# Fetching a block's V rows in turn with the next block's U rows

## The chip, the cores and the metric

The kernel runs on one core of a Trainium2 chip. Times are device microseconds (us) of one execution. The engines are PE (TensorE, matrix products; PEld is its weight load), DVE (VectorE), ACT (ScalarE), POOL (GpSimd) and SP (SyncE). SP issues the plain loads from HBM, POOL the indirect ones, which gather rows by an index; 16 DMA engines move both. Each engine runs its own instructions in the order in which they were placed, and waits for the others by semaphores.

## The reference

The reference is two model blocks, one after the other, over 256 tokens of width 1024. What matters here is the product-key retrieval that closes each layer of the first block. Every token picks 128 experts (8 heads of 16) out of 16384; its hidden vector is multiplied with the 128 rows `u_tab[e]`, and the results weigh the 128 rows `v_tab[e]`:

```python
def block(hb):                       # 128 tokens
    ...
    e = i1 * N_KEYS + i2             # n, 8 heads, 16 experts
    g = jax.nn.softmax(sc.astype(jnp.float32), axis=-1).astype(hb.dtype)
    a = jax.nn.gelu(jnp.einsum('nhkd,nd->nhk', u_tab[e], hb)) * g
    return jnp.einsum('nhk,nhkd->nd', a, v_tab[e])
```

In layer 0 it is done for the 256 latent tokens x and for the 256 context tokens xc; in layer 1 for x alone.

## The kernel before, in words

The kernel is unrolled. A scheduler orders each engine's instructions from the order of the program, so that code that is written in turn comes out roughly in turn. Layer 0's retrieval is `peer0`. It treats the two sets of tokens in two ways at once.

The latent tokens go densely. A main loop has 128 steps, called chunks here. Chunk c takes one tile of 512 KB of V (128 experts): ACT rounds it to `whi` (L349), DVE takes the rest `wlo` (L352), and PE adds 12 products into `ps_acc`. Until chunk 76 it takes one tile of U as well, 52 chunks ahead (`ps_U`, 8 products, then ACT's Gelu into `A`, L1377). The weights that pick the experts, `ps_G`, are made beside it on DVE and PE, in four bursts. A third strand, `ps_ada`, makes layer 1's modulations from loads `raw<-in_wada`. SP loads all these through four buffers `raw`.

The context tokens go by gathering, in the generator `gathered`, two blocks of 128 tokens. First come the dots: for each of 128 experts of a token, POOL gathers the row of U for the 128 tokens of the block into a buffer (L1289), and DVE multiplies it with the tokens' hidden vectors `ht` and sums (L1303). Then a Gelu, a product and a transpose give the weights `aT`. Last come the sums: for each token POOL gathers its 128 rows of V (512 KB as well), and PE multiplies them with a column of `aT` that DVE has put into `Z`, 4 products into `ps_gv`. After 32 tokens ACT copies `ps_gv` into `yg` (L1329), PE transposes it (`ps_gT`) and DVE adds it to the context.

The gathered rows go into a ring of buffers, `st["buf"]`: four `gb` to begin with, and the two tiles `ht` when the dots that read them are done. Gather number n takes buffer n modulo the length of the ring, and waits until that buffer's last reader is through. `peer0` calls the generator 2.1 times beside every chunk's U part and 2.1 times beside its V part (`UNITS`), so 4.2 steps a chunk until chunk 76 and 2.1 after it. There are 512 steps: 256 dots and 256 sums. Layer 1's `peer1` uses the same generator with one block.

Of the kernel before, what the change touches and what calls it, by code (L numbers as in the profile page):

```python
# [7 lines left out]
FT = mybir.dt.float32  # L8
# [3 lines left out]
OP = mybir.AluOpType  # L12
# [5 lines left out]
P = 128  # L18
# [278 lines left out]
class Kern:  # L297
# [995 lines left out]
    def gathered(self, st, l, s, nb):  # L1293


        nc, pe = self.nc, self.pe
        U, V = self.A[f"Ur{l}"], self.A[f"V{l}"].rearrange("a b d -> (a b) d")
        x = self.X if s else self.XC
        aT = []
        for b in range(nb):  # L1300
            for j in range(P):
                t = self.rows_of(st, U, st["e"][:, b, j:j + 1])
                nc.vector.scalar_tensor_tensor(t, t, 1.0, st["ht"][:, b], op0=OP.mult, op1=OP.mult,  # L1303
                                               accum_out=st["d"][:, b, j:j + 1])
                yield
            d = st["d"][:, b]
            nc.scalar.activation(d, d, AF.Gelu_apprx_tanh)
            nc.vector.tensor_mul(d, d, st["g"][:, b])
            ps = self.psb("ps_aT")
            self.tr(ps[:, 0:P], d)  # L1310
            a = pe.tile([P, P], FT, tag="aT", bufs=2, name="aT")
            nc.scalar.copy(a, ps[:, 0:P])
            aT.append(a)
        st["buf"] += [st["ht"][:, b] for b in range(nb)]
        for g in range(nb * P // 32):
            po = self.psb("ps_gv")[:, :256]
            for k in range(32):
                t = 32 * g + k
                if t % self.NZ == 0:
                    z = st["Z"][t // self.NZ % 2]  # L1320
                    nc.vector.tensor_copy(z[:, :, 32:33], aT[t // P][:, t % P:t % P + self.NZ].unsqueeze(2))
                v = self.rows_of(st, V, st["eT"][:, t // P, t % P:t % P + 1])
                for q in range(4):
                    self.mm(po[32 * q:32 * q + 32], z[:, t % self.NZ, 32 - k:64 - k], v[:, q * 256:(q + 1) * 256],
                            k == 0, k == 31)
                yield

            y = pe.tile([P, 256], FT, tag="yg", bufs=1, name="yg")
            nc.scalar.copy(y, po)  # L1329
            pt = self.psb("ps_gT")  # L1330
            for c in range(2):
                self.tr(pt[:, c * P:(c + 1) * P], y[:, c * P:(c + 1) * P])
            for c in range(2):
                m = self.mods[l][:, 40 + c:48:2, s:s + 1].broadcast_to([P, 4, 32])
                xv = x[:, c::2, 32 * g:32 * g + 32]
                r = pe.tile([P, 4, 32], FT, tag="rg", bufs=2, name="rg")
                nc.vector.tensor_tensor(r, pt[:, c * P:(c + 1) * P].rearrange("p (q t) -> p q t", q=4), m, op=OP.mult)
                nc.vector.tensor_tensor(xv, xv, r, op=OP.add)
        self.gathered_all = True
        yield  # L1340

# [987 lines left out]
```

## Time and profile before

| | us |
|---|---|
| median of three runs | 3970.74 |
| lowest and highest | 3969.45, 3972.92 |
| profiled execution, its own time | 3959.87 |
| span of its trace | 3958.1 |
| PE busy | 3552.3 (90%) |
| DVE busy | 2345.2 (59%) |
| POOL busy | 1253.4 (32%) |

The span is read in 40 slices of 99 us. `peer0`'s main loop lies between 975 and 1940 us, in slices 10 to 19 (counted from 0), and is followed by a short rest of gathers until about 1980 us. In that stretch the DMA engines are busy most of the time, and DVE is busy first and idle later. A granted clock below 1.00 means that PE ran a part of that stretch at the lower of its two levels.

### The profile page before, as it was taken

The numbers are of one execution on the slowest core, as the hardware profiler recorded it, in microseconds if no ns is written. First come the engines' busy times: TensorE is split into PE (matmuls) and PEld (weight loads), VectorE is DVE, ScalarE is ACT, GpSimd is POOL, SyncE is SP. The second block draws the span as 40 slices with busy tenths as digits, with TensorE's granted clock in tenths as the row PEclk, the third lists the DMA queues.
The fourth block names the chain that finished last, engine by engine and source line by source line (L and its number), as shares of the span: only waits on it lengthen the run. The fifth ranks groups of instructions, "written<-read, shape, count | busy, mean of one in ns | idle before, by whom it ended". The sixth has DMA issues, their size and how long they took to land. (4 is left out here: it accounts for less than half of the span.)

```text
span 3958.1 us, 63943 instructions
## 1 busy us (share of the span) xinstructions
PE 3552.3 (90%) x24642; PEld 2838.3 (72%) x24642; DVE 2345.2 (59%) x5406; ACT 1201.6 (30%) x2156; POOL 1253.4 (32%) x1037
## 2 busy tenths in 40 slices
PE   8999996967898799899889996777999999999999
PEld 6777875755676566566489995673334899999899
DVE  5843358789687643165377448854201656865785
ACT  5433321111111111123265411110001646554554
POOL 0012204532534534455513204534432132231122
PEclk9999998987898999999999998899999999999999
DMA  5244237974989989899924468999998404565354
GB/s 214 66 158 149 91 113 250 336 248 139 364 315 351 371 296 333 313 335 391 373 91 160 147 213 306 344 409 396 409 409 333 149 25 137 181 203 172 99 178 147
DMA packets 265793, 961.39 MB, mean 243 GB/s; under 512 B 29832, under 2 KB 31504, under 8 KB 265488
## 3 DMA queue, kind: packets, MB, share of 16 engines
q1 hardware_dynamic: 154752, 554.08, 40.1%
q0 software_dynamic: 110592, 402.70, 27.0%
q8 instruction: 194, 3.18, 0.3%
q14 instruction: 111, 0.91, 0.1%
q10 hardware_dynamic: 144, 0.52, 0.0%
HBM read 956.12 MB, written 1.06 MB: 242 GB/s over the span
## 5 line engine op out<-in xcount | busy, mean ns | idle before, releaser
L322 PE MATMUL ps_U<-h,raw 128*128 128x256 f32 (+1 forms) x4096 | 758.0, 342 | 63.8 <-DMA raw<-in_U 37.5
L322 PEld LDWEIGHTS ps_U<-h,raw 128*128 128x128 f32 x4096 | 657.7, 201 | 145.4 <-ACT A L1485 36.1
L352 DVE TENSOR_TENSOR wlo<-raw,whi 128x1024 fp32r<-128x1024 f32 (+1 forms) x409 | 503.4, 1232 | 420.1 <-ACT whi L349 418.6
L349 ACT CAST whi<-raw 128x1024 fp32r<-128x1024 f32 (+1 forms) x502 | 517.7, 1034 | 751.0 <-DMA raw<-in_V 340.4
L1289 POOL DMA_INDIRECT gb<-in_Ur,er x384 | 469.2, 1222 | 856.4 <-DVE gb L1303 441.0
L1303 DVE SCALAR_TENSOR_TENSOR gb<-gb,ht 128x1024 f32<-128x1024 f32 x384 | 466.3, 1226 | 223.3 <-DMA gb<-in_Ur,er 222.4
L352 POOL TENSOR_TENSOR wlo<-raw,whi 128x1024 fp32r<-128x1024 f32 (+1 forms) x93 | 222.0, 2387 | 929.0 <-ACT whi L349 733.0
L1289 POOL DMA_INDIRECT gb<-in_V,eT x280 | 291.9, 1042 | 329.9 <-PE ps_gv L322 286.3
L322 PE MATMUL ps_in<-hh_hi,whi 128*128 128x256 f32 (+1 forms) x776 | 267.2, 347 | 1.7 <-ACT hh_hi L567 1.7
L322 PE MATMUL ps_in<-hh_hi,wlo 128*128 128x256 f32 (+1 forms) x776 | 262.7, 339 | 1.1 <-POOL wlo L352 1.1
L322 PE MATMUL ps_in<-hh_lo,whi 128*128 128x256 f32 (+1 forms) x776 | 263.5, 340 | 0.1
L322 PE MATMUL ps_acc<-raw,A 128*128 128x512 f32 x512 | 256.1, 621 | 8.0 <-DMA raw<-in_V 7.8
L322 PE MATMUL ps_acc<-wlo,a_hi 128*128 128x512 f32 x512 | 216.7, 423 | 45.3 <-DVE wlo L352 45.1
L322 PE MATMUL ps_acc<-whi,a_hi 128*128 128x512 f32 x512 | 220.0, 437 | 12.4 <-ACT whi L349 12.4
L322 PE MATMUL ps_acc<-whi,a_lo 128*128 128x512 f32 x512 | 211.9, 414 | 0.0
L322 PE MATMUL ps_gv<-gb,Z 128*32 128x256 f32 x2240 | 172.5, 398 | 9.6 <-DMA gb<-in_V,eT 8.9
L322 PE MATMUL ps_q<-h,raw 128*128 128x256 f32 x768 | 176.3, 382 | 0.0
L322 PEld LDWEIGHTS ps_acc<-raw,A 128*128 128x128 f32 x512 | 86.5, 190 | 121.4 <-issue 78.8
L322 PEld LDWEIGHTS ps_in<-hh_hi,whi 128*128 128x128 f32 x776 | 147.7, 191 | 27.3 <-issue 8.4
L1289 POOL DMA_INDIRECT ht<-in_V,eT x104 | 111.8, 1075 | 163.3 <-PE ps_gv L322 143.1
L322 PEld LDWEIGHTS ps_in<-hh_hi,wlo 128*128 128x128 f32 x776 | 147.3, 190 | 19.4 <-POOL wlo L352 1.9
L322 PEld LDWEIGHTS ps_in<-hh_lo,whi 128*128 128x128 f32 x776 | 147.6, 190 | 15.8 <-DVE hh_lo L570 0.3
(627 smaller groups left out, 7335.5 us busy)
## 6 DMA issues: line engine op xcount, KB each, us to landing
raw<-in_U SPq DMA_DIRECT2D x256, 512.0 KB, 6.8
raw<-in_V SPq DMA_DIRECT2D x256, 512.0 KB, 7.5
raw<-in_win SPq DMA_DIRECT2D x96, 512.0 KB, 4.0
raw<-in_wup SPq DMA_DIRECT2D x88, 512.0 KB, 4.2
raw<-in_wada SPq DMA_DIRECT2D x80, 512.0 KB, 5.1
raw<-in_wq SPq DMA_DIRECT2D x48, 512.0 KB, 4.1
raw<-in_gwin SPq DMA_DIRECT2D x37, 512.0 KB, 3.5
raw<-in_wdn SPq DMA_DIRECT2D x32, 512.0 KB, 4.3
```

Of the source, the lines that this page charges most:

```text
L322: self.nc.tensor.matmul(o, l, r, start=start, stop=stop)
L349: nc.scalar.copy(hi[:, :f], raw[:, :f])
L352: eng.tensor_sub(lo[:, :f], raw[:, :f], hi[:, :f].bitcast(FT))
L1289: self.nc.gpsimd.indirect_dma_start(t, None, table, bass.IndirectOffsetOnAxis(ap=at, axis=0), bounds_check=P * P - 1, oob_is_err=False)
L1303: nc.vector.scalar_tensor_tensor(t, t, 1.0, st["ht"][:, b], op0=OP.mult, op1=OP.mult, accum_out=st["d"][:, b, j:j + 1])
```

## The change

`gathered` is cut into two inner generators, `dots(b)` and `sums(b)`. Block 0's dots run first, as before. Then one step of block 1's dots and one step of block 0's sums are taken in turn, 128 pairs. Then come block 1's sums. The numbers of gathers, of products and of steps stay what they were. `ht` of block 0 joins the ring after block 0's dots (five buffers), `ht` of block 1 after block 1's (six). With one block (`peer1`) nothing changes.

```diff
         aT = []
-        for b in range(nb):
+
+        def dots(b):
             for j in range(P):
                 t = self.rows_of(st, U, st["e"][:, b, j:j + 1])
...
             aT.append(a)
-        st["buf"] += [st["ht"][:, b] for b in range(nb)]
-        for g in range(nb * P // 32):
-            po = self.psb("ps_gv")[:, :256]
...
+            st["buf"].append(st["ht"][:, b])
+
+        def sums(b):
+            for g in range(4 * b, 4 * b + 4):
+                po = self.psb("ps_gv")[:, :256]
...
+        yield from dots(0)
+        last = sums(0)
+        for b in range(1, nb):
+            d = dots(b)
+            while True:
+                n = 0
+                for q in (d, last):
+                    if next(q, self) is not self:
+                        n += 1
+                        yield
+                if n == 0:
+                    break
+            last = sums(b)
+        yield from last
         self.gathered_all = True
```

What this does to the order on the engines is seen at three places. The first is POOL, where the gathers of the context stand one behind the other. `in_Ur` is the table of U's rows and `in_V` that of V's; `gb` and `ht` are the buffers. Before:

```order
L1289 DMA gb<-in_Ur,er 128x1024 x134
L1289 DMA ht<-in_V,eT 128x1024
L1289 DMA gb<-in_Ur,er 128x1024 x122
L1289 DMA gb<-in_V,eT 128x1024 x3
L1289 DMA ht<-in_V,eT 128x1024
```

And now:

```order
L1289 DMA gb<-in_Ur,er 128x1024 x129
L1289 DMA gb<-in_V,eT 128x1024
L1289 DMA gb<-in_Ur,er 128x1024 x2
L1289 DMA ht<-in_V,eT 128x1024
L1289 DMA gb<-in_V,eT 128x1024 x3
L1289 DMA ht<-in_Ur,er 128x1024
L1289 DMA gb<-in_Ur,er 128x1024 x2
L1289 DMA ht<-in_V,eT 128x1024
```

From the 130th on gathers of V stand among those of U: of the eleven shown behind the 129, six are of V, and fill buffers that only PE empties.

The second place is DVE just after the dots of block 0, at chunk 6: `dots<-dots,gr` is the product after that block's Gelu, `wlo`, `a_lo` and `adar` belong to the dense work. Before:

```order
L1308 TENSOR_TENSOR dots<-dots,gr 128x128
L1303 SCALAR_TENSOR_TENSOR gb,dots<-gb,ht 128x1024
L352 TENSOR_TENSOR wlo<-raw,whi 128x1024
L363 TENSOR_TENSOR a_lo<-A,a_hi 128x256
L1303 SCALAR_TENSOR_TENSOR gb,dots<-gb,ht 128x1024 x4
L363 TENSOR_TENSOR a_lo<-A,a_hi 128x256
L352 TENSOR_TENSOR wlo<-raw,whi 128x1024
L1303 SCALAR_TENSOR_TENSOR gb,dots<-gb,ht 128x1024 x2
```

And now:

```order
L1309 TENSOR_TENSOR dots<-dots,gr 128x128
L352 TENSOR_TENSOR wlo<-raw,whi 128x1024
L363 TENSOR_TENSOR a_lo<-A,a_hi 128x256
L1304 SCALAR_TENSOR_TENSOR gb,dots<-gb,ht 128x1024 x2
L363 TENSOR_TENSOR a_lo<-A,a_hi 128x256
L352 TENSOR_TENSOR wlo<-raw,whi 128x1024
L441 TENSOR_TENSOR adar<-adar,ps_ada 128x256
L363 TENSOR_TENSOR a_lo<-A,a_hi 128x256
L352 TENSOR_TENSOR wlo<-raw,whi 128x1024
L441 TENSOR_TENSOR adar<-adar,ps_ada 128x256
```

The order goes on like this until chunk 16: at the 15th `wlo` 160 dots stand behind DVE before and 131 now; at the 25th it is 179 and 145, at the 45th 256 and 187. The first `ps_gv` stands on PE at chunk 47 before and at chunk 17 now, in both cases just behind the transpose `ps_aT`.

The third place is PE at chunk 70, with `ps_gv` as the sums, `ps_gT` as the transpose that follows 32 tokens, and between these rows the 12 products `ps_acc` of a chunk. Before:

```order
L322 MATMUL ps_gv<-gb,Z_3989 32x256 x8
L322 MATMUL ps_U<-h_3864,raw 128x256 x8
L327 MATMUL ps_gT<-cst,yg 128x128 x2
L322 MATMUL ps_gv<-ht,Z_3988 32x256 x8
L322 MATMUL ps_acc<-whi,a_hi 128x512
```

And now:

```order
L322 MATMUL ps_gv<-gb,Z_3989 32x256 x4
L322 MATMUL ps_U<-h_3864,raw 128x256 x8
L322 MATMUL ps_gv<-gb,Z_3988 32x256 x4
L322 MATMUL ps_acc<-whi,a_hi 128x512
```

Half the sums stand there, and no transpose: it now stands at chunks 32, 48, 63 and 79 instead of 55, 63, 70 and 79. In ACT's order the copy `yg` of chunk 70 stood behind the 73rd `whi`; the copies now at 32, 48, 63 and 79 stand behind the 33rd, 48th, 65th and 82nd, those before at 55, 63 and 79 behind the 56th, 65th and 82nd. The order of SP's loads is the same in both kernels, and from chunk 80 on the counts of sums at each chunk are too.

## Rows read from the trace of the kernel before

**Rows 1.** The page: the span in 40 slices, busy tenths.

```profile
PE   8999996967898799899889996777999999999999
DVE  5843358789687643165377448854201656865785
DMA  5244237974989989899924468999998404565354
```

**Rows 2.** Stretches of `peer0`: PE, PEld, DVE, ACT, POOL busy (count), PEclk, DMA share, GB/s.

```profile
1020.00:1130.00 110.00, 94.09 (x559) 72.29 (x559) 81.26 (x172) 20.62 (x37) 52.67 (x40) 0.91 0.94 345
1130.00:1200.00 70.00, 68.18 (x592) 53.93 (x591) 61.97 (x158) 15.35 (x29) 22.57 (x17) 1.00 0.90 314
1200.00:1400.00 200.00, 164.31 (x883) 124.73 (x881) 141.43 (x274) 38.70 (x69) 97.08 (x76) 0.91 0.93 352
1400.00:1700.00 300.00, 270.30 (x2254) 189.86 (x2250) 100.21 (x242) 51.91 (x93) 120.26 (x115) 0.95 0.88 322
1717.00:1940.00 223.00, 222.01 (x1965) 145.52 (x1967) 133.28 (x305) 71.59 (x108) 119.03 (x107) 1.00 0.98 374
```

**Rows 3.** The same stretches, tile `ps_acc` alone: PE busy (count) first.

```profile
1020.00:1130.00 110.00, 43.99 (x136) 28.97 (x135) 0.00 (x0) 0.00 (x0) 0.91 0.94 345
1130.00:1200.00 70.00, 28.02 (x108) 19.62 (x108) 0.00 (x0) 0.00 (x0) 1.00 0.90 314
1200.00:1400.00 200.00, 77.00 (x243) 51.51 (x241) 0.00 (x0) 0.00 (x0) 0.91 0.93 352
1400.00:1700.00 300.00, 93.34 (x348) 67.10 (x348) 0.00 (x0) 0.00 (x0) 0.95 0.88 322
```

**Rows 4.** Waits, 1000 to 1400 us: total, times, longest.

```profile
PE ps_acc L322 <- DVE wlo L352: 45.1, 27, 4.8
...
DVE gb L1303 <- DMA gb<-in_Ur,er: 71.2, 49, 3.7
...
POOL gb L1289 <- DVE gb L1303: 172.9, 89, 6.4
```

**Rows 5.** The dots on DVE, whole run: ns minimum, median, maximum.

```profile
L1303 DVE SCALAR_TENSOR_TENSOR gb<-gb,ht x384: 1202/1224/1742, 630.2 to 2726.9; 128x1024 f32<-128x1024 f32 x192
L1303 DVE DVE_READ_ACCUMULATOR gb<-gb,ht x384: 73/82/88, 631.3 to 2728.1; 128x1 f32 x192
```

**Rows 6.** Gathers on POOL, 1130 to 1200, then 1200 to 1400 us: ns.

```profile
L1289 POOL DMA_INDIRECT gb<-in_Ur,er x17: 1027/1732/1736, 1135.3 to 1199.7; - x17
...
L1289 POOL DMA_INDIRECT gb<-in_Ur,er x71: 984/992/2014, 1199.7 to 1368.8; - x71
```

**Rows 7.** The stretch 1400 to 1700 us, tile `ps_gv` alone: PE, PEld, ACT.

```profile
1400.00:1700.00 300.00, 62.87 (x936) 24.80 (x936) 1.10 (x3) 0.95 0.88 322
```

**Rows 8.** Waits of PE's weight loads, 1400 to 1700 us.

```profile
PEld ps_gv L322 <- issue: 19.2, 57, 0.7
```

**Rows 9.** Timeline of PE, 1638 to 1659 us: start, length, what [idle before].

```profile
1638.63 3.72 PE L322 MATMUL ps_U<-h,raw 128*128 128x256 f32 x16
1657.42 0.69 PE L327 MATMUL ps_gT<-cst,yg 128*128 128x128 f32 x2 [15.07 <-ACT yg L1329]
```

**Rows 10.** Timeline of ACT over the same time.

```profile
1648.99 1.04 ACT L349 CAST whi<-raw 128x1024 fp32r<-128x1024 f32 x1 [10.30 <-DMA raw<-in_V]
...
1656.05 1.04 ACT L349 CAST whi<-raw 128x1024 fp32r<-128x1024 f32 x1 [5.43 <-DMA raw<-in_V]
1657.00 0.37 ACT L1329 COPY yg<-ps_gv 128x256 f32<-128x256 f32 x1
```

**Rows 11.** DMA issues, 1000 to 1400, then 1700 to 2010 us: us to landing.

```profile
gb<-in_Ur,er POOLq DMA_INDIRECT x134, 7.2
...
gb<-in_V,eT POOLq DMA_INDIRECT x90, 8.0
```

More of the change, by code (lines that the diff above doesn't have):

```diff
@@ L1313, in gathered @@
             aT.append(a)
-        st["buf"] += [st["ht"][:, b] for b in range(nb)]
-        for g in range(nb * P // 32):
-            po = self.psb("ps_gv")[:, :256]
[L1317 to L1338, printed above, removed]
@@ new lines, in dots @@
+            st["buf"].append(st["ht"][:, b])
+        def sums(b):
+            for g in range(4 * b, 4 * b + 4):
+                po = self.psb("ps_gv")[:, :256]
+                for k in range(32):
+                    t = 32 * g + k
+                    if t % self.NZ == 0:
+                        z = st["Z"][t // self.NZ % 2]
+                        nc.vector.tensor_copy(z[:, :, 32:33],
+                                              aT[t // P][:, t % P:t % P + self.NZ].unsqueeze(2))
+                    v = self.rows_of(st, V, st["eT"][:, t // P, t % P:t % P + 1])
+                    for q in range(4):
+                        self.mm(po[32 * q:32 * q + 32], z[:, t % self.NZ, 32 - k:64 - k],
+                                v[:, q * 256:(q + 1) * 256], k == 0, k == 31)
+                    yield
+                y = pe.tile([P, 256], FT, tag="yg", bufs=1, name="yg")
+                nc.scalar.copy(y, po)
+                pt = self.psb("ps_gT")
+                for c in range(2):
+                    self.tr(pt[:, c * P:(c + 1) * P], y[:, c * P:(c + 1) * P])
+                for c in range(2):
+                    m = self.mods[l][:, 40 + c:48:2, s:s + 1].broadcast_to([P, 4, 32])
+                    xv = x[:, c::2, 32 * g:32 * g + 32]
+                    r = pe.tile([P, 4, 32], FT, tag="rg", bufs=2, name="rg")
+                    nc.vector.tensor_tensor(r, pt[:, c * P:(c + 1) * P].rearrange("p (q t) -> p q t", q=4), m,
+                                            op=OP.mult)
+                    nc.vector.tensor_tensor(xv, xv, r, op=OP.add)
@@ L1339, in gathered @@
+        yield from dots(0)
[7 more added lines that the diff above has]
+                        n += 1
+                        yield
+                if n == 0:
+                    break
+            last = sums(b)
+        yield from last
         self.gathered_all = True
```

## The prediction

> **What bounds the kernel now.** I read the page's slices first, then the main loop of the layer-0 retrieval in stretches, then the waits and the timeline inside each. The slices [rows 1] show DMA at nine tenths nearly throughout the loop (slices 10 to 19), DVE high in its first half and low in its second. The dots are the first half, the sums the second, so the change moves DVE work later and PE work earlier; it removes no byte and no product. The stretches show what limits where [rows 2]; dividing the count of `ps_acc` products by 12 gives the chunks done in each [rows 3]:
>
> - A, 1020 to 1130 us: 136/12 = 11.3 chunks, 9.7 us each, 40 gathers. PE is idle 16 us and below full clock.
> - B, 1130 to 1200: 9.0 chunks, 7.8 us each, only 17 gathers, since a burst of `ps_G` work fills DVE. PE is busy 68.2 of 70 us at full clock: PE sets the pace.
> - C, 1200 to 1400: 20.25 chunks, 9.9 us each, 76 gathers.
> - D, 1400 to 1700: 29 chunks, 10.3 us each, 115 gathers, now sums.
>
> In A and C the dots set the pace: POOL waits 173 us for DVE to free a buffer, DVE waits 71 us for gathered rows to land, and PE waits 45 us for the `wlo` queued behind those dots [rows 4]. In D PE is busy 270 us of 300, with one hole of 15 us: PE stands at `ps_gT`, whose copy `yg` stands on ACT behind a `whi` that waits for its load [rows 9, 10].
>
> **The change stage by stage.** The stages are kept by their chunks, and the sum is made against the profiled execution (span 3958.1, its own time 3959.87). The three timed runs have a median 10.9 us above that; I add the difference to the median. A gather is 512 KB, 0.524 MB. A dot costs DVE 1.22 + 0.08 = 1.3 us [rows 5]; a step of the sums costs PE 62.87/(936/8) = 0.54 us [rows 7], and where it starts a run of its own, a gap of 19.2/57 = 0.34 us [rows 8].
>
> A: the order now has about two dots between chunks 6 and 16, because V rows fill the ring and PE's first `ps_gv` is at chunk 17. Some 32 of the 40 gathers go away from here. DVE loses 32 x 1.3 = 42 of its 81 us, DMA 17 of 38 MB. Then PE is the limit. Its granted clock of 0.91, between the levels 0.5 and 1 (1.2 and 2.4 GHz), means 18% of 110 us at half speed; at full speed its 94.1 us are 94.1 - 9.9 = 84. Ends: 84 (-26) and 110 (0). The nearest row is B's 7.8 us a chunk with few gathers, 88 us; with some 4 us for its first chunks, where the last dots still come, I take 92: -18.
>
> B: PE, already the limit, gets two steps a chunk, 18 x 0.54 = 10 us, and up to 18 x 0.34 = 6 us of gaps. The gathers go from 17 to about 34, so 22.0 MB become 30.9; at C's 352 GB/s that is 88 us, at D's 322 it is 96, at the 374 of the stretch behind D 83. Ends +10 and +26; I take +16, between PE's sum and DMA's at C's rate.
>
> C: DVE sheds about 32 dots (42 us), and with them most of the waits above. PE's 164.3 us, 18 less at full clock, get 42 steps (23 us) and gaps (14): 183. Gathers go from 76 to 85, so 70.4 MB become 75.1: 213 us at 352 GB/s, 201 at 374. Ends -17 and +13; I take 0, by the rate of 374, since the stall that held 352 down was DVE's and is gone.
>
> D: the sums there halve, 117 to 61 steps, 30 us less on PE; at full clock its 270 us would be 255 - 30 = 225. DMA's 96.6 MB stay: 300 us at 322 GB/s, 274 at 352, 258 at 374. The 15 us hole goes: `yg` then stood behind three more loads of V than PE had used (73 against 70), and at the new places behind none to three, as at 55, 63 and 79 before. Of those with such a lead only 79 remains, where no U is loaded. Ends 0 and -42; I take -18, the hole and a little of PE's relief.
>
> The weights of block 1 (`ps_aT`) now come at chunk 79, with `ps_gv` behind them. No PE wait of this kind stands in the rows; at worst PE waits for the last gather and its dot, 7.2 + 1.3 us [rows 5, 11]. I take +4 of 0 to +8.5. From chunk 80 on, order and bytes are as before: 0.
>
> The extra PSUM bank that `ps_gv` holds from chunk 17 instead of 47 is costed at nothing: the sums ran with it beside the same `ps_U` and `ps_G` in D. If the cover fails, it is part of the ends of B and C.
>
> Sum: -18 + 16 + 0 - 18 + 4 = -16. As a test, B to D move 203 MB in 86 + 200 + 282 = 568 us, 357 GB/s, between C's 352 and the next stretch's 374. Ends together: -75 and +47.
>
> One row speaks against the move: in B a gather's issue takes 1732 ns on POOL against 992 in C [rows 6], where the `ps_G` work runs on DVE. 34 gathers at that price and some 0.3 us between them are 69 us, inside B's 86; with the longest issue of these rows, 2.01 us, 79, still inside. The Trainium skill (SBUF — State Buffer, "SBUF: two separate sides") says that DVE in a two-port mode locks GpSimd out, so that it can't write the descriptors of its DMAs; the trace agrees in direction, 1732 against 992 ns. The same page ("A bandwidth-pool intuition that's wrong") gives some 3100 ns for a DMA so blocked; by that, as an estimate, B would take 34 x 3.4 = 116 us, +46 instead of +16, and the sum would be +14. No gather in these rows takes that long.
>
> **Rivals.**
>
> 1. The shared ring sets the pace, slower. With five buffers a gather of U reuses a slot that PE must empty, and a gather of V one that DVE must empty, both through one POOL queue. One round (sum, gather of U, dot, gather of V, sum) spans five pairs, and takes two issues and landings, 2 x (1.0 to 1.7 + 7.2 to 8.0) [rows 6, 11], 1.3 + 0.54 of work, and the wait for a turn: half of the 4.8 us between two places of `ps_gv`, and about one `wlo` or dot on DVE. That is 22 to 25 us, and at 2.1 pairs a chunk 9.2 to 10.5 us a chunk, against 570/58.3 = 9.8 now in B to D. At 10.5 they take 612 us: -18 + 42 + 4 = +28, 3999. The point from which it decides is 24 us a round (10.1 a chunk), where A's gain is used up. For it: DVE already waited 71 us for a ring of four. Against it: D ran sums on a ring of six with PE nearly full.
> 2. DMA takes it back, no change. A to D move 227 MB in 680 us, 334 GB/s. What A doesn't move comes later, and if the mean rate stays, the end stays: 3971. For it: shares of 0.88 to 0.94 in all four. Against it: 374 GB/s right after them.
> 3. DMA runs at 374 from B on: 203 MB in 543 us instead of 570, A at 88 us: -27 - 22 + 4 = -45, 3926. For it: DVE no longer holds the buffers. Against it: two engines now have to empty them in turn. The Trainium skill (DMA: Bandwidth & Descriptors, "Specifications") puts a core's share of HBM at about 358 GB/s; by that 203 MB need 567 us, as in my sum, and this rival falls. The trace disagrees: 374 GB/s as the mean of 223 us [rows 2].
>
> That the change does nothing is excluded by the order of POOL.
>
> **How the numbers follow.** Forecast 3971 - 16 = 3955, chance 0.38, with a range of its own of 3935 to 3962. Rival 3 has 0.15, rival 2 0.26, rival 1 0.21. What this measurement can tell from no change is 0.2%, 8 us. The forecast and rival 3 lie below that: faster 0.53. Rival 2 lies within: 0.26. Rival 1 lies above: 0.21. For 8 in 10 I go from rival 3's price, 3926, to two thirds of rival 1's, 3990.
>
> **What would show it.** A: hardly a gather between chunks 6 and 16, a chunk at 8 us or less, a clock nearer 1. B: a chunk at 9.5. C and D: 9.6 to 9.9, with DVE's waits for gathers under half of 71 us, no PE hole of 15 us, and 350 GB/s or more. I am wrong if A doesn't quicken, if POOL waits long for `ps_gv` or the dots while DMA falls under 340 GB/s in C and D (rival 1), or if holes at the new `ps_gT` or at chunk 79 cost more than 8 us.

## The result and the profile after

The changed kernel takes 4024.26 us (median of 4 runs, 4022.34 to 4029.59) against 3971.83 for the kernel before, a ratio of 1.0130 with a 95% interval of 1.0117 to 1.0144. It is 52 us slower; I had forecast 16 us faster. The profiled execution (its own time 4026.07, span 4023.9) stands 66 us above that of before, since that one lay 12 us under its median. The stages below are told against these two.

The page of the kernel after, its span in 40 slices as in [rows 1], now of 100.6 us each:

```profile
PE   8999996867998889889989996777999999999999
DVE  6833368788564366456458547854200666865785
DMA  6244237964789888889944467999999413565254
```

DVE is less busy in slices 10 to 13 (6, 8, 7, 6 before) and more in 14 to 16 (4, 3, 1 before), as the order said. But DMA, which stood at 9, 8, 9, 8, 9 in slices 13 to 17, now stands at 8 in all five, and PE is at 8 in five of the six slices from 12 to 17.

The same stretches as in [rows 2], kernel after; PE, PEld, DVE, ACT, POOL busy (count), granted clock, DMA share, GB/s:

```profile
1020.00:1130.00 110.00, 103.32 (x728) 80.22 (x727) 52.42 (x129) 25.38 (x46) 13.12 (x13) 0.98 0.68 243
1130.00:1200.00 70.00, 61.64 (x527) 44.10 (x526) 49.37 (x131) 10.97 (x20) 28.26 (x28) 0.98 0.92 340
1200.00:1400.00 200.00, 167.40 (x1025) 114.73 (x1024) 90.07 (x181) 32.95 (x61) 93.33 (x77) 0.90 0.89 333
1400.00:1700.00 300.00, 255.61 (x1856) 178.40 (x1855) 168.05 (x367) 49.25 (x88) 140.88 (x114) 0.91 0.86 321
```

And `ps_acc` alone, as in [rows 3], with 1700 to 1800 us as a last row:

```profile
1020.00:1130.00 110.00, 42.21 (x158) 29.88 (x159) 0.00 (x0) 0.00 (x0) 0.98 0.68 243
1130.00:1200.00 70.00, 22.71 (x83) 15.92 (x81) 0.00 (x0) 0.00 (x0) 0.98 0.92 340
1200.00:1400.00 200.00, 70.61 (x216) 48.25 (x216) 0.00 (x0) 0.00 (x0) 0.90 0.89 333
1400.00:1700.00 300.00, 98.17 (x324) 67.48 (x324) 0.00 (x0) 0.00 (x0) 0.91 0.86 321
1700.00:1800.00 100.00, 39.86 (x146) 27.46 (x146) 0.00 (x0) 0.00 (x0) 0.93 0.83 309
```

That last row in the kernel before:

```profile
1700.00:1800.00 100.00, 59.52 (x228) 41.06 (x228) 0.00 (x0) 0.00 (x0) 1.00 0.93 338
```

Divided by 12 these are 13.2 chunks in A for 11.3 before: A gained, with 13 gathers for 40. From there on the kernel is slower: 6.9 chunks for 9.0 in B, 18 for 20.25 in C, 27 for 29 in D, and 12.2 for 19 in the 100 us behind D. There the turns and the U tiles go on until about 1760 us in the new kernel, while in the old the U tiles end at 1712 us and only sums are left.

What is waited for from 1000 to 1400 us, as in [rows 4] (total, times, longest):

```profile
DVE gb L1304 <- DMA gb<-in_Ur,er: 95.8, 37, 8.4
POOL gb L1289 <- DVE gb L1304: 82.8, 33, 7.3
POOL ht L1289 <- PE ps_gv L322: 82.3, 2, 81.3
...
PE ps_acc L322 <- DVE wlo L352: 31.6, 16, 5.3
DVE ht L1304 <- DMA ht<-in_Ur,er: 30.0, 11, 6.8
```

The wait of 81.3 us is the change at work: a gather of U, into a buffer `ht` that holds a row of V, stands at the head of POOL's queue until PE has done its first sum, at 1118 us, and so A has 13 gathers. The first and the last row are the trouble: DVE waits 126 us for rows of U where it waited 71, in a stretch that has fewer dots (DVE is busy 90 us of C for 141). The timeline of POOL at 1643 us shows why. Columns: start, length, what, [idle before and what ended it].

```profile
1643.71 1.73 POOL L1289 DMA_INDIRECT gb<-in_V,eT  x1 [4.96 <-DVE gb L1304]
1645.75 0.99 POOL L1289 DMA_INDIRECT gb<-in_Ur,er  x1 [0.30 <-issue]
1647.05 0.99 POOL L1289 DMA_INDIRECT gb<-in_V,eT  x1 [0.30 <-issue]
1648.35 0.99 POOL L1289 DMA_INDIRECT ht<-in_Ur,er  x1 [0.30 <-issue]
1653.88 1.73 POOL L1289 DMA_INDIRECT gb<-in_V,eT  x1 [4.54 <-DVE gb L1304]
```

DVE and then PE over the same time:

```profile
1642.21 1.23 DVE L1304 SCALAR_TENSOR_TENSOR gb<-gb,ht 128x1024 f32<-128x1024 f32 x1 [5.26 <-DMA gb<-in_Ur,er]
1643.36 0.08 DVE L1304 DVE_READ_ACCUMULATOR gb<-gb,ht 128x1 f32 x1
1643.36 1.22 DVE L352 TENSOR_TENSOR wlo<-raw,whi 128x1024 fp32r<-128x1024 f32 x1
...
1652.37 1.23 DVE L1304 SCALAR_TENSOR_TENSOR gb<-gb,ht 128x1024 f32<-128x1024 f32 x1 [6.16 <-DMA gb<-in_Ur,er]
1653.52 0.08 DVE L1304 DVE_READ_ACCUMULATOR gb<-gb,ht 128x1 f32 x1
```

```profile
1640.43 0.64 PE L322 MATMUL ps_gv<-gb,Z 128*32 128x256 f32 x8
```

Each gather takes buffer n modulo 5, and with five buffers and two tables in turn a gather of V always follows a row of U in its buffer. The gather of V at 1643.71 waits for a dot, which ends at 1643.44. The gather of U behind it, at 1645.75, needs a buffer that PE emptied at 1641.07, but it stands in the same queue: it goes 4.7 us after that. Its row lands 5.6 us after the issue, DVE has idled 6.2 us for it, its dot ends at 1653.60, and 0.28 us later the next gather of V goes. That is a closed loop of 10.17 us: V's issue 1.73 and 0.31, U's issue 0.99, landing 5.63, dot 1.23, hand-over 0.28. It spans two pairs of gathers, since the scheduler has put V's gather one place ahead of where the program writes it: V's waits for dot k, and U's k+2 is right behind it. A pair takes 5.1 us so, and at 2.1 pairs a chunk 10.7 us a chunk, where the kernel before took 9.8 in B to D. Over the whole of 1200 to 1700 us there are 191 gathers, 5.24 us a pair. The loop is not this one place: in these 500 us POOL stands 43 times over 2.5 us before a gather of V with DVE as the releaser, and the median from one such wait to the next is 11.2 us.

### The profile page after: what moved, and what is told of

Same layout as the page of the kernel before. It is cut to its first block, busy times and chain, and to the rows that moved or that the text cites. A ratio compares the mean times of both kernels' runs of the same rounds, so it can differ in the third digit from the quotient of the medians.

```text
span 4023.9 us, 63899 instructions
## 1 busy us (share of the span) xinstructions
PE 3582.7 (89%) x24642; PEld 2838.6 (71%) x24642; DVE 2346.7 (58%) x5406; ACT 1200.3 (30%) x2156; POOL 1260.4 (31%) x1037
## 5 line engine op out<-in xcount | busy, mean ns | idle before, releaser
L1304 DVE SCALAR_TENSOR_TENSOR gb<-gb,ht 128x1024 f32<-128x1024 f32 x359 | 438.2, 1226 | 391.4 <-DMA gb<-in_Ur,er 382.0
L1289 POOL DMA_INDIRECT gb<-in_Ur,er x359 | 427.3, 1190 | 730.6 <-DVE gb L1304 293.6
L1289 POOL DMA_INDIRECT gb<-in_V,eT x298 | 330.3, 1108 | 465.5 <-PE ps_gv L322 197.2
L322 PE MATMUL ps_acc<-whi,a_hi 128*128 128x512 f32 x512 | 222.8, 443 | 10.1 <-ACT whi L349 10.1
L322 PE MATMUL ps_gv<-gb,Z 128*32 128x256 f32 x2384 | 194.5, 405 | 21.7 <-DMA gb<-in_V,eT 21.3
L322 PEld LDWEIGHTS ps_gv<-gb,Z 128*32 128x32 f32 x2384 | 52.6, 110 | 171.0 <-issue 95.0
L322 PEld LDWEIGHTS ps_acc<-wlo,a_hi 128*128 128x128 f32 x512 | 104.1, 203 | 86.7 <-DVE wlo L352 66.1
L322 PEld LDWEIGHTS <-P 128*128 128x128 f16 x2560 | 86.4, 100 | 107.5 <-DVE Pg L1240 71.1
```

The lines of the kernel that those rows point to most:

```text
L322: self.nc.tensor.matmul(o, l, r, start=start, stop=stop)
L1289: self.nc.gpsimd.indirect_dma_start(t, None, table, bass.IndirectOffsetOnAxis(ap=at, axis=0), bounds_check=P * P - 1, oob_is_err=False)
```

## The experiments

All ratios are to runs of the kernel before on the same chip, with 95% intervals. Chunks are `ps_acc` products over 12. A few records can be missing, so they are good to a per cent or so. Where the dots end early in the 500 us, only sums are left, at 2.1 gathers a chunk for 4.2, so there gathers and GB/s tell less than chunks. That holds for e1 to e4, whose last row of U is gathered at 1480, 1592, 1620 and 1448 us (1767 in the changed kernel).

| kernel | ratio | chunks 1020-1130 | chunks 1200-1700 | gathers 1200-1700 | GB/s there |
|---|---|---|---|---|---|
| before | 1 | 11.3 | 49.2 | 191 | 334 |
| after | 1.0130 (1.0117 to 1.0144) | 13.2 | 45.0 | 191 | 326 |
| e1, parted 3 U, 2 V | 1.0020 (1.0007 to 1.0032) | 11.1 | 50.4 | 185 | 336 |
| e2, parted 2 U, 3 V | 1.0061 (1.0042 to 1.0079) | 11.8 | 47.1 | 187 | 329 |
| e3, four shared | 1.0147 (1.0119 to 1.0175) | 11.5 | 45.0 | 183 | 318 |
| e4, six shared | 0.9979 (0.9965 to 0.9993) | 10.2 | 53.0 | 184 | 335 |
| e8, short dots | 1.0117 (1.0094 to 1.0140) | 12.0 | 41.0 | 174 | 297 |
| e11, before, five and seven | 0.9969 (0.9957 to 0.9981) | 12.2 | 51.3 | 194 | 337 |
| e12, program's order | 0.9988 (0.9972 to 1.0003) | 13.2 | 51.8 | 215 | 364 |
| e13, V held ahead | 1.0179 (1.0155 to 1.0203) | 13.0 | 43.9 | 183 | 315 |
| e14, e13 with short dots | 0.9933 (0.9909 to 0.9957) | 13.1 | 46.9 | 196 | 333 |
| e15, program's order, six | 0.9909 (0.9891 to 0.9927) | 14.0 | 51.0 | 212 | 360 |
| e16, e12 again | 0.9980 (0.9967 to 0.9993) | 13.6 | 50.9 | 212 | 358 |

**e1 to e4: which buffers.** My theory after the result: the odd shared ring ties dots and sums together through POOL's queue. Its rivals: five buffers are too few for two strands (capacity), or gathering from two tables lowers what DMA can move (mixing).

e1 parts the five buffers while turns are taken, e2 the same with 2 and 3:

```diff
-        t = st["buf"][st["n"] % len(st["buf"])]
-        st["n"] += 1
+        r = st.get(kind)          # "u" or "v"; None outside the turns
...
+            st["u"], st["v"] = st["buf"][:3], st["buf"][3:]
```

> The changed kernel, but during the mixed steps the same five buffers are split: three take only rows of U (emptied by DVE), two only rows of V (emptied by PE). Theory T (the odd shared ring chains the two strands: a gather of V waits for a dot, the next gather of U stands behind it in POOL's queue, so only two rows of U are in flight and a pair takes 5.2 us): the U strand is free, the V strand takes 4.3 to 5.5 us a pair, so 3975 us, between 3950 and 4000. Rival C (five buffers are too few for two strands, however shared): 4024, within 10. Rival M (mixing the strands caps DMA near 320 GB/s, whatever the buffers): 4024, within 10.

> As the split of three and two, but two buffers for U and three for V. Theory T: two rows of U in flight, but no V issue in their loop: (1.3 + 0.3 + 1.2 + 6.3)/2 = 4.6 us a pair instead of 5.2, so 3985 us, between 3960 and 4005. Rivals C and M: 4024, within 10.

e3 keeps four shared buffers until all dots are done; e4 takes four slots from the ring of the dense part (`RING0`) for a sixth buffer:

```diff
-            st["buf"].append(st["ht"][:, b])
+            if b == nb - 1:
+                st["buf"] += [st["ht"][:, i] for i in range(nb)]
```

```diff
-    RING0 = 52
+    RING0 = 48
...
+        sc["buf"] += [pe.tile([P, D], FT, name=f"gx{i}") for i in range(1)]
```

> The changed kernel with one buffer less in the mixed steps: the tile ht of block 0 joins the ring only with that of block 1. With four shared buffers a gather of U takes over from U and one of V from V, two each, so the strands are not chained. Theory T: fewer buffers are no slower: 4000 us, between 3970 and 4030. Rival C: a buffer is held 13.1 us on average (26.2 us for five pairs), so four give 6.5 us a pair instead of 5.2, 128 pairs, +165: near 4190, in any case above 4080. Rival M: 4024 or a little more.

> The changed kernel with one buffer more (six shared in the mixed steps, so three for each strand and no chain); its space comes from U's lead over V, 48 chunks instead of 52. Theory T: no ring binds, 9.3 to 9.6 us a chunk by PE and DMA instead of 10.7 over 62 chunks: 3945 us, between 3925 and 3970. Rival C: 6 buffers held 13.1 us, 4.4 us a pair, the same 3945. Rival M: 4024, within 15. The lead of 48 instead of 52 may cost something by itself; both kernels will be run with it.

e1 came to its number (1.0020): with the same five buffers, bytes and dots it is 44 us under the changed kernel by the ratios, though it has A's gain no more (11.1 chunks there). Capacity and mixing, which put it at 4024, fall. e2 gains less (1.0061): with two buffers its rows of U come at 22 in 100 us from 1200 to 1400, for 27 in e1, and DVE waits 95 us for them there, for 55. e3 is the test of capacity: one buffer fewer costs next to nothing (1.0147 for 1.0130). In an even ring a buffer comes back to its own table, and the two strands do run apart here: the dots end 147 us earlier than in the changed kernel. e4 beat the kernel before. DMA was not capped by the mix; the stretch 1200 to 1400 us of e4:

```profile
1200.00:1400.00 200.00, 171.06 (x1174) 117.65 (x1166) 118.00 (x246) 31.94 (x60) 114.21 (x95) 0.96 1.01 389
```

But the gain of e4 may come from the room or from the turns. The controls are `RING0 = 48` alone in the kernel before (e5) and in the changed one (e7), and e4's two edits in the kernel before (e6):

> The kernel before with four slots fewer in the ring of the dense part (RING0 48 for 52: U's tiles run 48 chunks ahead for 52, 16 KB a partition freed), nothing put into the room. It is the control for the runs with an extra buffer. If the lead of the dense part doesn't matter (theory): within 8 us of before. If the four slots are worth time by themselves: over 10 us away, in either direction, and the runs with the extra buffer have to be read against this one.

> The kernel before with RING0 48 and one buffer more for the gathered rows: five for the dots, seven for the sums, no turn-taking. Theory (with rows of one table alone every slot waits for one engine, and five already cover a gather's landing): DVE's waits for gathered rows in 1000 to 1400 us (71 us before) fall under half, and the time is 5 to 25 us under before, 3945 to 3965. Rival (the extra buffer helps only where the two tables are mixed): within 8 us of before. If it is also below the turn-taking kernel with six buffers (ratio 0.998), taking turns is worth nothing even with a ring that is long enough.

> The changed kernel with RING0 48 and no extra buffer: the control for the run with six. Theory (the sixth buffer made the 66 us, not the room it was taken from): 4015 to 4035, a pair of gathers still takes 5.1 to 5.4 us. Rival (the shorter lead of the dense part made it): about 3960.

e5 (before, `RING0` 48) gave 1.0077 (1.0049 to 1.0105): the four slots cost some 30 us by themselves, which I had not expected. e7 (after, `RING0` 48) gave 1.0165 (1.0144 to 1.0187), so the sixth buffer made e4 and not the shorter ring. e6, the kernel before with five buffers for its dots, gave 0.9952 (0.9935 to 0.9969). So the kernel before was short of buffers too: its dots waited for their own ring, and with the fifth buffer DVE waits 31 us for rows of U from 1000 to 1400 us, for 71. Once more e4 (as e10) and e6 (as e11) side by side, and with them e9, e4 with e1's edit, its six parted four (`[:4]`) to two (`[4:]`):

> The changed kernel with RING0 48 and one buffer more, and the six buffers of the turns parted: four for U's rows, two for V's (against the shared six, which are three and three). Theory (each strand's pace is its hold time over its buffers): U's gathers every 2.6 to 3.3 us (3.6 with three), V's 4.5 to 5.0 us (4.4 with three), the dots end some 40 us earlier and the sums fall back; 3945 to 3970, ratio 0.996 to 1.002. Rival (it was only the total of six that counted): the same time and periods as with six shared, within 5 us.

> The changed kernel with RING0 48 and six shared buffers again, beside the next one on one chip. Theory: ratio 0.996 to 1.000. If taking turns is worth something once the ring is long enough, it is under the kernel before with the same room by more than 8 us.

> The kernel before with RING0 48 and five buffers for the dots again, beside the one above. Theory (the room was worth it and the turns were not): ratio 0.993 to 0.997, and 5 to 15 us below the turn-taking kernel with the same room. Rival: the two are within 8 us, and the difference between the two earlier calls came from the chip.

e9 gave 0.9974 (0.9961 to 0.9987), e10 0.9968 (0.9956 to 0.9980), e11 0.9969 (0.9957 to 0.9981). e9 went against my theory: parted four to two is the same as shared, and from 1200 to 1400 us its rows of U come as often as with three (28 in 100 us in both). So with six the hold time over the number of buffers no longer sets the pace; what does was not looked for. e10 and e11 are equal: the gap between e4 and e6 does not come back side by side, and with this order the turns are worth nothing beyond the room.

**e12: the order alone.** If the loop is what I say, it needs no buffer to open it. e12 adds an edge from each gather to the one that the program writes before it, with no semaphore:

```diff
+        i = self.nc.gpsimd.indirect_dma_start(t, None, table, ...
...
+        if st.get("last") is not None:
+            self.tc.add_manual_dep(i.ins, st["last"].name, mybir.DependencyInfo(
+                mybir.DependencyClass.NoSync, mybir.DependencyReason.DATA), reason="program order")
+        st["last"] = i.ins
```

> The changed kernel with its five shared buffers, and POOL held to the order in which the program writes the gathers (U, V, U, V). In the changed kernel as it stands each gather of V is moved one place forward: V's waits for dot k, and U's k+2 stands right behind it; held to the program's order the row behind it is U's k+3, so that the same loop (dot, issue of V, issue of U, landing, dot; 10.4 us) spans three pairs for two. Theory (the loop through POOL's queue sets the pace): a pair takes 3.5 to 4.5 us for 5.24, PE or DMA sets the pace then, and the time is 3945 to 3985. Rival (five slots for two strands are too few in whatever order): 4010 to 4035. Rival (held to this order POOL waits for PE's sums instead): over 4035.

In the two traces ACT and SP run in the same order to the last instruction, and so does PE, but for two records of 24642 that stand swapped; POOL differs at 230 of 1037 places and DVE at 56 of 5406. The ratio fell from 1.0130 to 0.9988. Its stretches 1200 to 1400 and 1400 to 1700 us:

```profile
1200.00:1400.00 200.00, 177.08 (x1163) 120.27 (x1162) 100.99 (x200) 35.14 (x65) 97.86 (x85) 0.97 0.98 368
1400.00:1700.00 300.00, 273.01 (x1993) 192.52 (x1991) 180.92 (x383) 55.75 (x102) 153.72 (x131) 0.97 0.96 361
```

DMA went from 333 and 321 GB/s to 368 and 361 with the same buffers. POOL at about the same time:

```profile
1641.18 0.99 POOL L1289 DMA_INDIRECT gb<-in_V,eT  x1 [2.20 <-DVE gb L1308]
1642.47 1.00 POOL L1289 DMA_INDIRECT gb<-in_Ur,er  x1 [0.30 <-issue]
1643.78 0.99 POOL L1289 DMA_INDIRECT gb<-in_V,eT  x1 [0.30 <-issue]
1645.23 1.31 POOL L1289 DMA_INDIRECT gb<-in_Ur,er  x1 [0.47 <-PE ps_gv L322]
```

Longer gaps are not gone, but over the 500 us there are 10 above 4 us, for 25 in the changed kernel, and of the 43 waits of V for DVE over 2.5 us 8 are left. What is waited for from 1200 to 1400 us, in the changed kernel and then in e12:

```profile
DVE gb L1304 <- DMA gb<-in_Ur,er: 75.0, 25, 8.4
POOL gb L1289 <- DVE gb L1304: 58.0, 16, 7.3
POOL gb L1289 <- PE ps_gv L322: 3.5, 5, 2.1
```

```profile
POOL gb L1289 <- PE ps_gv L322: 60.5, 31, 6.4
DVE gb L1308 <- DMA gb<-in_Ur,er: 26.0, 17, 4.9
POOL gb L1289 <- DVE gb L1308: 15.0, 9, 5.3
```

POOL now waits for PE's sums. A pair takes 4.65 us, more than the 3.5 to 4.5 that I expected; the time is inside its range. By the ratios 56 us of the changed kernel's time (60 by e16 below) lay in the order of one queue.

**e8, e13, e14: is the dot in the loop?** e8 shortens the dots:

```diff
-                nc.vector.scalar_tensor_tensor(t, t, 1.0, st["ht"][:, b], ...
+                nc.vector.scalar_tensor_tensor(t[:, 0:128], t[:, 0:128], 1.0, st["ht"][:, b, 0:128], ...
```

> The changed kernel with each dot over 128 of the 1024 columns, in both layers (7/8 of every dot is left out), so that a dot takes DVE about 0.2 us for 1.2. Theory (a loop over two pairs: the dot frees U's slot, then V's issue, then U's issue, landing, dot): the loop loses 1.0 us every two pairs, a pair goes from 5.24 to about 4.7 us, and the 128 pairs save about 65 us; with what DVE's relief gives in the first dots (up to 40 us) the time is 3920 to 3965. Rival (a round over five pairs, as the prediction put it: one dot in each five pairs): a pair goes to about 5.0 us, 25 us saved, with the first dots 3960 to 4000. Rival (a U gather waits mainly for PE's sums, DVE is not in the loop): the pair stays at 5.2 us, only the first dots gain, 3980 to 4024.

Its time, 4012.94 us, is that of the last rival, its pairs are nobody's: from 1200 to 1700 us gathers came slower than with whole dots.

```profile
1200.00:1700.00 500.00, 392.17 (x2599) 270.12 (x2599) 156.25 (x496) 74.65 (x135) 202.33 (x174) 0.89 0.83 297
```

174 gathers are 5.75 us a pair, for 5.24. The run does not answer its question, because the scheduler, which orders by its own estimate of durations, had put POOL's gathers two by two (V, V, U, U). e13 therefore holds POOL to one order, the changed kernel's, written out: V's gather j right ahead of U's 128+j, with the same buffer for every row as there. e14 is e13 with the short dots, and its order of the gathers is e13's.

```diff
+        n = st["n"] + (kind == "v")
+        t = st["buf"][n % len(st["buf"])]
+        st["n"] += {None: 1, "v": 0, "u": 2}[kind]
...
-                for q in (d, last):
+                for q in (last, d):
```

> The changed kernel, the same buffers for the same rows, and POOL held to the order V, U, V, U in which V's gather j stands right ahead of U's 128+j all through the turns: V's waits for U's dot k, and U's k+2 stands behind it, the loop over two pairs in its pure form, and the control for the next run. Theory: as the changed kernel, which has this order at 110 of its 128 places, or a little slower: 4015 to 4055. Rival (holding POOL to any fixed order gives the 60 us that the program's order gave): 3945 to 3985.

> e13_held with each dot over 128 of the 1024 columns, in both layers (7/8 of every dot is left out), and the same order of gathers as there. Theory (the dot is a part of the loop): the loop of two pairs loses 0.9 us, a pair 0.45, some 110 pairs 50 us; the dots of the first block, which stand in DVE's way, and those of layer 1 give 20 to 45 more: 70 to 95 us under e13_held. Rival (the loop runs over issues and landings alone, a dot lies beside them): 20 to 45 us under e13_held, and the pair of gathers keeps its time.

Both as the theory had it. e13 is slower than the changed kernel (1.0179): a fixed order by itself gives nothing, it has to be the right one. Of e13, then e14, 1200 to 1700 us:

```profile
1200.00:1700.00 500.00, 412.04 (x2821) 285.40 (x2821) 253.44 (x545) 79.31 (x142) 213.49 (x183) 0.91 0.85 315
```

```profile
1200.00:1700.00 500.00, 423.01 (x2847) 294.15 (x2845) 165.49 (x519) 84.30 (x152) 219.37 (x196) 0.94 0.89 333
```

A pair goes from 5.46 to 5.10 us (0.36; I had said 0.45), and the time falls by 96 us (4046.87 to 3950.45; I had said 70 to 95). In this stretch chunks come at 10.7 us for 11.4, some 45 us over the 62 chunks of the turns; the rest lies outside the turns: at 1020 us e14 is 4 chunks ahead, by the first block's dots, and behind the main loop it gains 19 us more. The median from one long wait of V for DVE to the next falls from 11.2 to 10.5 us. So the dot is a part of the loop, beside issue and landing, which make the larger part. Shorter dots also let `wlo` go earlier; what that alone gives was not tried apart.

**e15, e16: what the change is worth without the loop.** e16 is e12 again; e15 is e12 with e4's six buffers.

> The changed kernel in the program's order of gathers as e12, with RING0 48 and six shared buffers. Theory (with six no gather waits for the other table's reader, so the order matters little): within 8 us of six buffers in the scheduler's order (0.997), 3940 to 3960. Rival (order and sixth buffer add up): under 3935.

> e12 again with more rounds: the changed kernel, five shared buffers, the program's order of gathers. If the prediction's terms are right apart from the loop: 0.996 (16 us under before). If DMA takes back what the first stage gains: 0.999 to 1.001.

e16 gave 0.9980 (0.9967 to 0.9993): faster by some 8 us (3 to 13), half of my sum. e15 gave 0.9909, 3937.92 us beside 3973.82: the fastest of all, and 24 us under the 0.997 that I expected of it. Order still matters with six, and beside the kernel before with the same room (e11, 0.9969, on another chip) the turns are then worth some 24 us. A, of e4 and then of e15:

```profile
1020.00:1130.00 110.00, 84.37 (x458) 63.73 (x457) 68.30 (x135) 19.83 (x35) 42.98 (x35) 0.89 0.86 310
```

```profile
1020.00:1130.00 110.00, 108.55 (x791) 83.25 (x791) 57.09 (x138) 26.37 (x46) 19.42 (x16) 0.99 0.72 260
```

In e4 the scheduler's order lets U's gathers pass those of V that wait for the first sum, and 35 of them stay in A: 10.2 chunks there. In e15 they stand behind it, and A runs 14.0 chunks with PE busy 108.6 of 110 us. The 3.8 chunks are some 37 us at 9.8 each, more than the 24 between the two; e4 gets a part back behind A (53.0 chunks for 51.0). This is read from the rows and was not tried apart.

## Why the prediction was wrong, point by point

Mechanism and sign were those of my rival 1, to which I had given 0.21; the time lies outside the range. Each stage is the prediction's chunks at the pace measured after.

- **A, -18:** right. 11.3 chunks at 110/13.2 = 8.4 us are 95 us, -15. The clock rose from 0.91 to 0.98 and the gathers fell to 13.
- **B, +16:** nearly. 9 chunks at 70/6.9 = 10.1 us are 91, +21.
- **C, 0:** wrong. 20.25 chunks at 11.1 us are 225, +25.
- **D, -18:** wrong. 29 chunks at 11.1 us are 322, +22. Of the waits of PE from 1400 to 1700 us the one for `yg`, the hole of 15 us in [rows 9], is down to 9.0:

```profile
PE ps_acc L322 <- DVE wlo L352: 17.7, 11, 2.9
PE ps_gT L327 <- ACT yg L1333: 9.0, 1, 9.0
```

  But that and PE's relief were worth nothing, since PE no longer set the pace.
- **`aT` and what follows, +4:** not as thought. No wait of PE for `ps_aT` stands in the rows from 1700 us on. The rest is 66 - 53 = +13; it was not parted further, but the last row of U is gathered at chunk 77, so the loop lasts beyond D's 75.

The failing step is the rate at which C and D were priced. I wrote that the stall that held C at 352 GB/s "was DVE's and is gone" and gave B to D 234 gathers in 568 us, 2.43 us each. The stall was not DVE's work: with the same dots and a fifth buffer the kernel before (e11) did 22.3 chunks in C for 20.25, at 362 GB/s. It was a gather waiting for a buffer, and the change made each such wait longer (POOL waited for dots in C 53 times for 77 us, and now 20 times for 72). DVE's wait for rows of U was to fall under half of 71 us and rose to 126. The gathers came every 500/191 = 2.62 us, no faster than before. That rate was to be had: e12's 215 gathers are 2.33 us each, at 364 GB/s, and e16's 212 are 2.36; by e16's ratio that kernel takes 3964 us beside 3971.83, where 3955 was forecast. With the loop open the stages come near their prices: by e12's rows A -15, B +17, C +2, D -27, by e16's -18, +24, +3, -19, where I had -18, +16, 0, -18. So the stages were sound in the main, though the whole gave half of the 16 us, and what I had not priced was one place in POOL's queue. The granted clock, 0.90 in C and 0.91 in D, stayed below the full clock of my sums for PE, but PE was idle 33 of the 200 and 44 of the 300 us, so it was not the limit.

Rival 1 had the right parts but not the right circle. I put the round through five buffers and five pairs, sum, U, dot, V, sum, at 22 to 25 us, and then asked whether it was longer than DMA's pace. The trace shows a shorter circle that needs no sum: a gather of V waits for a dot, and the gather of U that feeds the dot after next stands behind it in the queue. It takes 10.17 us for two pairs, 25.4 for five. That is above the 24 us that I named as the point from which it decides, and with the other waits it came to 26.2 (five pairs of 5.24). What spoke against it, D's sums on a ring of six with PE nearly full, was no evidence: there every buffer was emptied by the same engine, so no gather stood behind one that waited for another engine. And the order of POOL was before me, with V's gathers ahead of the U's that the program writes first; I read there how many of each stand where, and not which buffer each one waits for.

My reading of [rows 6] was wrong too, in a remark that gave no term of the sum: it put the long issues down to `ps_G` work, and they belong to the dots (last section).

Rival 2 (DMA's mean rate stays) comes near in its rate, 326 GB/s for 334 from 1200 to 1700 us, but not in the time, nor in the reason: shares of 0.86 to 0.89 were idle time, as e12's 0.98 and 0.96 show. Rival 3 (374 GB/s from B on) is not reached by e12 or e15, at 364 and 360 over the same 500 us.

## What to carry to other kernels

Where two strands with different readers share a ring of buffers and one issue queue, number the transfers, write beside each the reader that frees its buffer, and follow the queue: a transfer that waits for reader X must not stand ahead of the one that feeds X. A ring whose length is a multiple of the turn, parted rings, or an edge that holds the queue to the written order each open the loop, the last without a byte of memory (four shared buffers opened it too, but left each table only two). Such a loop's price is at least its length over the number of turns that it spans (10.2 us over two pairs here, over three in e12, where PE's sums then set the pace), so one place in the order can be worth nearly as much as a buffer: 56 to 60 us here, where the sixth buffer gave 74 to 78 (e7 against e4 and e10).

## What the runs showed of the hardware

A gather's issue takes 0.99 to 1.00 us on POOL when DVE stands idle beside it. If a dot or a `wlo` (1.22 us each) is already running on DVE when the issue begins, the issue ends 0.86 to 0.87 us after that instruction does. From 1000 to 1950 us this held for all 110 such issues of the changed kernel (DVE's instruction begun over 0.06 us before, with over 0.13 us left), for all 115 of the kernel before and all 111 of e12. Two stand above: at 1643.71, 1.73 us long, beside the `wlo` that runs from 1643.36 to 1644.58, and at 1653.88. Of the other 236 issues of the changed kernel 8 took over 1.2 us.

In the loop this comes at the worst place. The dot that releases POOL also frees DVE, which is 0.35 us into its next instruction when the issue begins; so 26 of the 43 long-awaited gathers of V took over 1.6 us, and it makes 0.74 of the 10.17 us. It also puts [rows 6] right: the nine gathers of 1.73 us in B of the kernel before each began 0.35 us into a dot, and the eight between them, with `ps_G` work beside them, took 1.03 to 1.11. So it was the dots, and not the `ps_G` work, that made them long.

DMA moved 389 GB/s as a mean of 200 us in e4 (396 in e9), above the 374 from which I had taken the upper end.
